# Probability-value products in runs of up to five key blocks, with the meta keys padded to 128

## The chip, the cores and the metric

One Trainium2 chip, one core used. The metric is the device time of one execution in microseconds (us). The profile is one execution of the same program, taken by the hardware profiler; times inside it count from the start of its span. Engines are PE (TensorE matmul), PEld (its weight loads), DVE (VectorE), ACT (ScalarE), POOL (GpSimd) and SP (which issues the DMAs).

## The reference, cut to what matters

Two layers of a streaming encoder. Each layer normalises, projects, runs three head groups (gated convolution, latent attention, RWKV-7) and projects back. Only the attention is touched here:

```
ckv_all = concat([ckv_past, rmsnorm(ckv)])            # KV_LORA = 128
kv = (ckv_all @ w_ukv).reshape(b, sk, 8, 64 + 64)      # per head: key part, value part
s = (q_nope . k_nope + q_rope . k_rope) * scale        # 8 heads
s = where(k_chunk <= q_chunk, s, -1e30)                # block-causal, chunks of 64
p = softmax(s)
o = p @ v                                              # 64 values per head
y_b = o * silu(gb)
```

The prompt has 16 meta tokens and 1024 frames. The sample has 64 new frames on 256 cached rows. Meta tokens and past are visible to every later query of their stream.

## The kernel before

Features lie on partitions and the 1104 tokens (64 sample, 16 meta, 1024 prompt) along the free axis. A layer has an input projection (`inproj`, `inproj_rest`), the attention and recurrence streams, and an output projection in two halves: `outproj_first` takes the first four of eight feature tiles, `outproj` the last four, which are the attention's.

Heads are taken in four pairs `pr`, queries in five units `u`: unit -1 holds the 64 sample and 16 meta queries, units 0 to 3 hold 256 prompt queries each. For a unit and each of its two heads:

- `scores` (L764) multiplies queries with keys into PSUM tiles `sc`. DVE takes the row maximum (`st`), ACT exponentiates into `p` (queries on partitions, keys along the free axis), DVE scales by the reciprocal of the sum.
- `transpose` (L831) turns `p` block by block so that keys lie on partitions. One block is one job of `jobs(u)` (L822): up to four PE transposes (two heads by two halves of the queries) into one PSUM tile `tr`, which `evict` (L665) copies to an SBUF tile `pt`, on ACT or DVE, whichever the planner has free sooner.
- `outputs` (L854) multiplies each `pt` with the value block `v` into the unit's only PSUM tile `po`: two matmuls per job, one per head, each with 64 columns of `v` as a 128x64 operand, into partitions 0 to 63 and 64 to 127. DVE then multiplies `po` with the gate into `yo`, and SP stores it to `yd`.

Unit u of the prompt has 2u + 3 jobs: the meta keys (16 partitions), 2u + 1 full blocks of 128 keys and a last block for the second half of the queries. Unit -1 has two. That makes 26 jobs a pair, 208 in both layers.

Which step comes next is decided when the program is built. `race` (L277) keeps the streams in the order `ORDER` = transpose, outputs, prepare, scores, and takes the first whose needs are met by the planner's clock; `fill` (`outproj_first`) goes where none is. `prepare` makes keys, values and queries of the pairs (`upk`, `val`, `upq`). A step's needs stand in its `yield`: tiles, PSUM tags, conditions. `outputs` yields once per job, as soon as one transposed tile waits. `transpose` may be ahead of `outputs` by fewer than `JOBS` = 3 tiles. `pt` tiles come from the ring `tmp` of four, which `qt` and `yraw` share. PSUM has two banks for `tr` (the 16-column score pieces use them too), one for `po`.

The trace puts all instructions on line L79, the helper that records every operation, so tiles tell them apart. An fp32 matmul stands in the trace as two PE rows, a transpose as one: a job of 256 queries is `tr` x4 and `po` x4.

Of the kernel before, what the change touches and what calls it, by code (L numbers as in the profile page):

```python
# [22 lines left out]
NMETA = 16  # L23
# [16 lines left out]
TURNS = ("sc", "tr", "sc", "tr", "po")  # L40
NEG = -1e30
PROBS = 8
JOBS = 3
LEAN = 0.1
POOL = 100.0
HOLD = 7
# [144 lines left out]
class Net:  # L191
# [421 lines left out]

    def value_tiles(self):
        vt = [self.S("x1", "v") for _ in range(2)]
        self.v = [vt[b < 4][:, 128 * (b % 4 if b < 4 else b - 4):128 * (b % 4 if b < 4 else b - 4) + 128] for b in range(12)]
        self.vs = lambda b, m: vt[b < 4][:, 128 * (b if b < 4 else b - 4):128 * ((b if b < 4 else b - 4) + m)]

# [89 lines left out]
    def attention(self, l):  # L708
# [6 lines left out]
        qa, keyed, valued, pt, turned, gates = {}, set(), set(), {}, [], {}  # L715
        count = {"scored": 0, "begun": 0, "p": 0, "out": 0, "jobs": 0}
# [105 lines left out]
        def jobs(u):  # L822

            if u < 0:
                n = PAD0
                return [[(0, 128, 0, n, 0, True, False), (1, 128, 2 * n, n, 0, False, False)], [(2, n, 0, n, 0, False, True)]]
            x = [[(3, NMETA, 0, 256, 0, True, False)]]
            x += [[(4 + k, 128, 0, 256, 0, False, False)] for k in range(2 * u + 1)]
            return x + [[(4 + 2 * u + 1, 128, 0, 128, 128, False, True)]]

        def transpose():  # L831
            for pr, u in units:
                yield (reached("scored", at[pr, u, 1] + 1),)
                ps2 = [pt[pr, u, j] for j in range(2)]
                q0, n = span(u)
                gates[pr, u] = self.small("gt", [128, 256], bufs=2)
                nc.sync.dma_start(gates[pr, u][:, :n], self.gd[2 + pr, :, q0:q0 + n])
                for js in jobs(u):
                    key = lambda b: (0, 128, PAST)[b] if u < 0 else 0 if b == 3 else NMETA + 128 * (b - 4)
                    yield lambda: len(turned) - count["jobs"] < JOBS, *ps2[0], *ps2[1], "tr"  # L840
                    ps = self.psa("tr", "tr")
                    for b, k, c, m, o, _, _ in js:
                        for j, p in enumerate(ps2):
                            for i, x in enumerate(p):
                                if o <= 128 * i:
                                    w, d = x.shape[0], c + j * m + 128 * i - o
                                    self.tr(ps[:k, d:d + w], x[:, key(b):key(b) + k], self.c(C_ID, w)[:w])
                    k, e = js[0][1], max(x[2] + 2 * x[3] for x in js)
                    t = self.tmp("pt")[:k, :e]
                    self.evict(t, ps[:k, :e])  # L850
                    turned.append(t)
                count["p"] -= len(ps2[0]) + len(ps2[1])

        def outputs():  # L854
            for pr, u in units:
                for x, js in enumerate(jobs(u)):
                    yield (lambda: len(turned) > count["jobs"] and all((pr, 4 * (b // 4) if b > 3 else 0 if b < 2 else b) in valued for b, *_ in js),)
                    t = turned[count["jobs"]]
                    yield t, *(self.v[b][:k] for b, k, *_ in js), *(("po",) if x == 0 else ())
                    if x == 0:  # L860
                        po = self.ps("po", "po")
                    for b, k, c, m, o, start, stop in js:
                        for j in range(2):
                            r = slice(64 * j, 64 * j + 64)
                            self.mm(po[r, o:o + m], self.v[b][:k, r], t[:, c + j * m:c + (j + 1) * m], start=start, stop=stop)
                    count["jobs"] += 1
                q0, n = span(u)
                yo = self.small("yo", [128, 256], bufs=2)
                nc.vector.tensor_tensor(out=yo[:, :n], in0=po[:, :n], in1=gates[pr, u][:, :n], op=ALU.mult)
                nc.sync.dma_start(self.yd[4 + pr, :, q0:q0 + n], yo[:, :n])  # L870
                count["out"] += 1
# [633 lines left out]
```

## Time and profile before

| | |
|---|---|
| median of 3 runs | 1581.6 us (1580.95 to 1582.13) |
| the profiled execution | 1581.68 us |
| its span | 1579.8 us |
| PE busy | 1522.3 us, 96% |
| DVE, ACT, POOL busy | 1040.9, 736.9, 276.2 us |
| granted TensorE clock, mean | 0.992 |

The attention streams' transposes and products run from 474 to 709 us in the first layer and from 1249 to 1483 us in the second. Before them lie the projections and the recurrence, behind them the second half of the output projection. PE is busy nearly all the time by its own rows, but the ends of matmuls are modelled and overlap, so a busy PE is not PE at its peak: the starts of the rows tell more than their durations. In a timeline row a run of like instructions is merged: its start, the time to its modelled end, and its count. In the rows by form, `128*64` is the weight operand's shape (partitions by columns), then comes the moving operand.

### The profile page before, as it was taken

The page shows a single profiled execution, that of the slowest core. Times are in us where ns is not written, and L with a number is a line of the kernel's source. Part 1 is how long each engine was busy: PE and PEld are TensorE (multiplying, and loading weights), DVE is VectorE, ACT ScalarE, POOL GpSimd, SP SyncE. Part 2 cuts the span into 40 slices and gives each one's busy share as a digit, 9 for nine tenths or more (in the row PEclk, how much of TensorE's full clock was granted, in tenths as well). Part 3 has the DMA queues.
Part 4 walks back from the last instruction along what each step waited for, and adds up shares of the span by engine and source line. Part 5 has one row for each costly group of instructions (what it writes and reads, how often), then busy time and mean ns, then how long its engine had stood idle before and what let it go on. Part 6 is the DMA issues. An engine that isn't in the chain of part 4 may idle for free. (4 is left out here: it accounts for less than half of the span.)

```text
span 1579.8 us, 31071 instructions
## 1 busy us (share of the span) xinstructions
PE 1522.3 (96%) x12304; PEld 1306.4 (83%) x12304; DVE 1040.9 (66%) x2591; ACT 736.9 (47%) x1730; POOL 276.2 (17%) x303
## 2 busy tenths in 40 slices
PE   7999999999999999999999999999999999999996
PEld 7988878888887767779999888798988867767896
DVE  7666575666758667755745675775666777666566
ACT  7135444324657556542522244434246666565342
POOL 0222222231211100100011222323122200100002
PEclk9999999999999999999999999999999999999998
DMA  6332122222224101112333312212312321012223
GB/s 213 121 102 77 42 66 51 76 47 87 77 85 144 36 25 32 58 45 87 128 108 101 108 43 53 81 38 72 67 47 93 120 93 45 17 32 68 69 64 115
DMA packets 95329, 119.84 MB, mean 76 GB/s; under 512 B 41872, under 2 KB 74768, under 8 KB 95184
## 3 DMA queue, kind: packets, MB, share of 16 engines
q1 hardware_dynamic: 95184, 117.87, 24.9%
q8 instruction: 96, 1.57, 0.4%
q14 instruction: 49, 0.40, 0.1%
HBM read 81.24 MB, written 36.60 MB: 75 GB/s over the span
## 5 line engine op out<-in xcount | busy, mean ns | idle before, releaser
L79 PE MATMUL prj<-hhi,whi 128*128 128x384 f32 (+1 forms) x1152 | 391.4, 340 | 7.4 <-ACT hhi L79 6.5
L79 PE MATMUL prj<-hhi,wlo 128*128 128x384 f32 (+1 forms) x1152 | 390.1, 339 | 0.9 <-DVE wlo L79 0.9
L79 PE MATMUL prj<-hlo,whi 128*128 128x384 f32 (+1 forms) x1152 | 387.7, 337 | 0.6 <-DVE hlo L79 0.6
L79 PEld LDWEIGHTS prj<-hhi,whi 128*128 128x128 f32 x1152 | 217.2, 189 | 12.5 <-ACT hhi L79 6.5
L79 PEld LDWEIGHTS prj<-hhi,wlo 128*128 128x128 f32 x1152 | 217.1, 188 | 6.1 <-DVE wlo L79 1.2
L79 PEld LDWEIGHTS prj<-hlo,whi 128*128 128x128 f32 x1152 | 217.4, 189 | 4.7 <-DVE hlo L79 1.0
L79 PE MATMUL prj<-yhi,wo 128*128 128x384 f32 (+2 forms) x776 | 199.4, 334 | 0.0
L79 ACT ACTIVATE p<-sc,st 128x144 f32<-128x144 f32 (+8 forms) x240 | 127.1, 536 | 79.3 <-DVE st L79 79.0
L79 PE MATMUL sc<-ka,qa 128*128 128x512 f32 (+9 forms) x720 | 150.5, 337 | 2.6 <-POOL qa L79 2.1
L79 PEld LDWEIGHTS prj<-yhi,wo 128*128 128x128 f32 x776 | 137.8, 188 | 2.6 <-issue 1.0
L79 DVE TENSOR_REDUCE st<-sc 128x1 f32<-128x144 f32 (+8 forms) x240 | 118.0, 501 | 23.0 <-PE sc L79 21.0
L79 PE MATMUL prj<-ylo,wo 128*128 128x384 f32 (+2 forms) x388 | 128.9, 332 | 0.0
L79 PEld LDWEIGHTS sc<-ka,qa 128*128 128x128 f32 (+1 forms) x720 | 112.0, 189 | 18.6 <-ACT p L79 3.6
L79 PE MATMUL tr<-cst,p 128*128 128x128 f32 (+3 forms) x752 | 122.0, 279 | 5.0 <-DVE p L79 4.3
L79 PEld LDWEIGHTS tr<-cst,p 128*128 128x128 f32 (+3 forms) x752 | 77.9, 132 | 51.8 <-issue 28.5
L79 ACT ACTIVATE pt<-tr 128x512 f32<-128x512 f32 (+4 forms) x158 | 84.6, 550 | 67.6 <-PE tr L79 66.7
L79 PE MATMUL po<-pt,v 128*64 128x256 f32 (+4 forms) x864 | 114.8, 365 | 0.9 <-DVE pt L79 0.8
L79 ACT ACTIVATE whi<-wraw 128x1024 fp32r<-128x1024 f32 x48 | 50.7, 1056 | 129.4 <-PE prj L79 119.8
L79 POOL TENSOR_TENSOR qa<-qt,qa 128x512 fp32r<-128x512 f32 (+1 forms) x40 | 48.0, 1211 | 350.3 <-ACT qa L79 261.7
L79 DVE TENSOR_TENSOR tri<-tri 48x14 f32<-48x14 f32 (+6 forms) x336 | 76.0, 226 | 17.1 <-DMA tri<-tri 7.3
L79 DVE TENSOR_SCALAR p<-p,st 80x336 f32<-80x336 f32 (+5 forms) x144 | 86.0, 600 | 1.4
L79 DVE TENSOR_TENSOR wlo<-wraw,whi 128x1024 fp32r<-128x1024 f32 x48 | 68.9, 1435 | 16.3 <-ACT whi L79 15.9
(223 smaller groups left out, 2606.8 us busy)
## 6 DMA issues: line engine op xcount, KB each, us to landing
wraw<-w_in SPq DMA_DIRECT2D x48, 512.0 KB, 3.7
wraw<-w_out SPq DMA_DIRECT2D x32, 256.0 KB, 2.6
zd<-z SPq DMA_DIRECT2D x14, 576.0 KB, 3.4
wr<-zd SPq DMA_DIRECT2D x36, 192.0 KB, 2.6
gd<-gate SPq DMA_DIRECT2D x12, 552.0 KB, 2.9
yraw<-yd SPq DMA_DIRECT2D x8, 552.0 KB, 4.0
xn<-x SPq DMA_DIRECT2D x8, 552.0 KB, 4.0
xd<-xn SPq DMA_DIRECT2D x8, 552.0 KB, 2.9
```

Of the source, the lines that this page charges most:

```text
L79: r = f(*args, **kw)
```

## The change

Four edits:

1. `outputs` no longer yields per job. The jobs of a unit are cut into batches of at most `BATCH` = 5, of near equal size (2; 3; 5; 4 and 3; 5 and 4 for the units -1 to 3), and a batch is issued in one run when all its transposed tiles and values are there.
2. The meta job transposes 128 columns of `p` instead of 16 and multiplies all 128 partitions with its value block.
3. `value_tiles` clears that value block once a layer (a POOL memset), so the 112 rows that are no meta keys add nothing.
4. `pt` gets a ring of its own of `JOBS` = 7 tiles, and `transpose` may be seven tiles ahead.

```
-JOBS = 3
+JOBS = 7
+BATCH = 5
...
         vt = [self.S("x1", "v") for _ in range(2)]
+        self.nc.gpsimd.memset(vt[1][:, 384:512], 0.0)
...
-            x = [[(3, NMETA, 0, 256, 0, True, False)]]
+            x = [[(3, 128, 0, 256, 0, True, False)]]
...
-                    t = self.tmp("pt")[:k, :e]
+                    t = self.small("pt", [128, 512], bufs=JOBS)[:k, :e]
...
-                for x, js in enumerate(jobs(u)):
-                    yield (lambda: len(turned) > count["jobs"] and all(... in valued for b, *_ in js),)
-                    t = turned[count["jobs"]]
-                    yield t, *(self.v[b][:k] for b, k, *_ in js), *(("po",) if x == 0 else ())
...
+                todo, po = jobs(u), None
+                while todo:
+                    size = -(-len(todo) // -(-len(todo) // BATCH))
+                    batch, todo = todo[:size], todo[size:]
+                    blocks = [b for js in batch for b, *_ in js]
+                    yield (lambda: len(turned) >= count["jobs"] + size and all(... in valued for b in blocks),)
+                    ts = turned[count["jobs"]:count["jobs"] + size]
+                    yield *ts, *(self.v[b][:k] for js in batch for b, k, *_ in js), *(() if po else ("po",))
+                    po = po or self.ps("po", "po")
+                    for t, js in zip(ts, batch):
+                        for b, k, c, m, o, start, stop in js:
...
+                    count["jobs"] += size
```

The program is built from this order, so the instructions of the attention stretch move on every engine. Ahead of the first attention unit the order is the old one.

PE before, first pair, unit 3: jobs of the long unit, where `tr` is a transposed block, `po` the unit's product, `p` the probabilities.

```order
L79 MATMUL po_5818<-pt_5777,v_5072 64x256 x2
L79 MATMUL tr_5821<-cst,p_5568 128x128
L79 MATMUL tr_5821<-cst,p_5598 128x128
L79 MATMUL tr_5821<-cst,p_5625 128x128
L79 MATMUL tr_5821<-cst,p_5716 128x128
L79 MATMUL po_5818<-pt_5784,v_5071 64x256 x2
L79 MATMUL tr_5830<-cst,p_5568 128x128
L79 MATMUL tr_5830<-cst,p_5598 128x128
L79 MATMUL tr_5830<-cst,p_5625 128x128
L79 MATMUL tr_5830<-cst,p_5716 128x128
L79 MATMUL po_5818<-pt_5816,v_5071 64x256 x2
```

Every transposed block is followed by one product; this goes on to the unit's last three, which stand together.

PE now, the same unit (its `po` has another number): the last block of the first batch, and the batch.

```order
L80 MATMUL tr_5912<-cst,p_5576 128x128
L80 MATMUL tr_5912<-cst,p_5674 128x128
L80 MATMUL tr_5912<-cst,p_5694 128x128
L80 MATMUL tr_5912<-cst,p_5727 128x128
L80 MATMUL po_5919<-pt_5783,v_5072 64x256 x2
L80 MATMUL po_5919<-pt_5790,v_5071 64x256 x2
L80 MATMUL po_5919<-pt_5831,v_5071 64x256 x2
L80 MATMUL po_5919<-pt_5849,v_5071 64x256 x2
L80 MATMUL po_5919<-pt_5895,v_5071 64x256 x2
```

Five products now stand in a row, the meta block's (`v_5072`) among them; the transposes of these blocks stand further ahead, among scores and fill.

PE now, a later unit of the fourth pair: `tr_7810` and `tr_7831` are given the same PSUM bank, `sc` are scores of another unit.

```order
L80 MATMUL tr_7810<-cst,p_7646 128x128
L80 MATMUL tr_7810<-cst,p_7666 128x128
L80 MATMUL tr_7810<-cst,p_7722 128x128
L80 MATMUL tr_7810<-cst,p_7742 128x128
L80 MATMUL sc_7846<-ka_4711,qa_7575 128x456
L80 MATMUL sc_7846<-ka_4712,qa_7575 128x456
L80 MATMUL sc_7846<-ka_4711,qa_7575 128x456
L80 MATMUL sc_7851<-ka_4711,qa_7575 128x456
L80 MATMUL tr_7831<-cst,p_7646 128x128
```

Between two tiles of one bank stand four score matmuls where before there stood another block's transposes and two products.

Counted in the whole program: `po` matmuls stand in 152 runs before (110 of them of one job) and in 70 now.

## Rows read from the trace of the kernel before

**Rows 1.** The page's first part: busy time and instructions of each engine.

```profile
PE 1522.3 (96%) x12304; PEld 1306.4 (83%) x12304; DVE 1040.9 (66%) x2591; ACT 736.9 (47%) x1730; POOL 276.2 (17%) x303
```

**Rows 2.** Busy time by stretch (both attentions): PE, PEld, DVE, ACT, POOL, clock, DMA.

```profile
480.00:700.00 220.00, 217.14 (x1528) 161.03 (x1527) 158.37 (x443) 130.91 (x367) 21.36 (x18) 0.99 0.18 55
1254.00:1474.00 220.00, 216.81 (x1527) 160.16 (x1527) 158.69 (x446) 131.24 (x368) 21.80 (x18) 1.00 0.18 55
```

**Rows 3.** Waits of PE, 474 to 709 us: total, times, longest.

```profile
PE tr L79 <- DVE p L79: 2.1, 4, 0.8
PE upq L79 <- ACT p L79: 1.3, 1, 1.3
PE sc L79 <- POOL qa L79: 0.9, 2, 0.6
PE po L79 <- DVE pt L79: 0.4, 1, 0.4
```

**Rows 4.** Timeline of all engines from 525.2 us: start, time, engine, operation, [idle before].

```profile
525.25 0.66 PE L79 MATMUL tr<-cst,p 128*128 128x128 f32 x4
525.83 0.20 PEld L79 LDWEIGHTS po<-pt,v 128*64 128x64 f32 x4 [0.17 <-issue]
525.83 0.65 PE L79 MATMUL po<-pt,v 128*64 128x256 f32 x4
525.94 0.60 ACT L79 ACTIVATE pt<-tr 128x512 f32<-128x512 f32 x1 [0.51 <-PE tr L79]
526.41 0.42 PEld L79 LDWEIGHTS tr<-cst,p 128*128 128x128 f32 x4 [0.39 <-issue]
526.42 0.66 PE L79 MATMUL tr<-cst,p 128*128 128x128 f32 x4
527.00 0.20 PEld L79 LDWEIGHTS po<-pt,v 128*64 128x64 f32 x4 [0.17 <-issue]
527.00 0.65 PE L79 MATMUL po<-pt,v 128*64 128x256 f32 x4
527.18 0.69 DVE L79 COPY pt<-tr 128x512 f32<-128x512 f32 x1 [1.69 <-PE tr L79]
```

**Rows 5.** Timeline of PE alone, five places: runs and what starts behind them.

```profile
487.93 1.23 PE L79 MATMUL po<-pt,v 16*64 16x256 f32 x8
489.09 0.52 PE L79 MATMUL sc<-ka,qa 128*128 128x264 f32 x2
...
499.76 1.49 PE L79 MATMUL sc<-ka,qa 128*128 128x456 f32 x6
501.09 0.20 PE L79 MATMUL sc<-hide 128*128 128x64 bf16 x1
501.22 0.87 PE L79 MATMUL po<-pt,v 128*64 128x256 f32 x8
502.02 0.50 PE L79 MATMUL sc<-ka,qa 128*128 128x16 f32 x3
...
518.24 0.82 PE L79 MATMUL tr<-cst,p 128*16 128x128 f32 x6
518.89 0.49 PE L79 MATMUL upk<-ckv,u 128*128 128x384 f32 x1
...
529.12 1.30 PE L79 MATMUL po<-pt,v 128*64 128x256 f32 x12
530.35 0.38 PE L79 MATMUL val<-u 128*128 128x128 f32 x1
```

**Rows 6.** Groups by form, whole span: count, busy us, mean ns, idle before.

```profile
L79 PE MATMUL tr<-cst,p 128*16 128x128 f32 x128 | 26.0, 273 | 2.5 <-DVE p L79 2.2
L79 PE MATMUL po<-pt,v 16*64 16x256 f32 x128 | 22.0, 400 | 0.0
L79 POOL MEMSET so<- 128x128 f32 x8 | 1.4, 203 | 0.0
```

**Rows 7.** The page's DMA issues: KB each, median us to landing.

```profile
wraw<-w_out SPq DMA_DIRECT2D x32, 256.0 KB, 2.6
```

More of the change, by code (lines that the diff above doesn't have):

```diff
@@ L855, in outputs @@
             for pr, u in units:
-                for x, js in enumerate(jobs(u)):
-                    yield (lambda: len(turned) > count["jobs"] and all((pr, 4 * (b // 4) if b > 3 else 0 if b < 2 else b) in valued for b, *_ in js),)
-                    t = turned[count["jobs"]]
-                    yield t, *(self.v[b][:k] for b, k, *_ in js), *(("po",) if x == 0 else ())
[L860 to L866, printed above, removed]
+                todo, po = jobs(u), None
[3 more added lines that the diff above has]
+                    blocks = [b for js in batch for b, *_ in js]
+                    yield (lambda: len(turned) >= count["jobs"] + size and all((pr, 4 * (b // 4) if b > 3 else 0 if b < 2 else b) in valued for b in blocks),)
+                    ts = turned[count["jobs"]:count["jobs"] + size]
[3 more added lines that the diff above has]
+                        for b, k, c, m, o, start, stop in js:
+                            for j in range(2):
+                                r = slice(64 * j, 64 * j + 64)
+                                self.mm(po[r, o:o + m], self.v[b][:k, r], t[:, c + j * m:c + (j + 1) * m], start=start, stop=stop)
+                    count["jobs"] += size
                 q0, n = span(u)
```

## The prediction

> **What bounds the kernel now.** I read the page's busy times first, then the stretches of the attention, then PE's waits there, then its timeline. PE is busy 96% of the span [rows 1]; in the two attention stretches it is 217 of 220 us, with the clock at 0.99 and 1.00, while DVE is busy 158 and ACT 131 [rows 2]. All waits of PE in the first layer's attention sum to 4.7 us [rows 3]. So PE's own order sets the time, and what is to be gained must lie inside "busy". The timeline shows where. A cycle of one transposed block and one product, from one `po` run to the next, takes 527.00 - 525.83 = 1.17 us [rows 4]. Read by starts, the same work needs less where like stands beside like: six transposes take 518.89 - 518.24 = 0.65, so 0.108 each and 0.43 for four; a run of three products (256, 256 and 128 queries) takes 530.35 - 529.12 = 1.23 and one of two (256 and 128) 502.02 - 501.22 = 0.80, so a product of 256 queries inside a run costs 0.43 [rows 5]. That makes 0.86. The missing 0.31 us is paid for going from transposes to products and back. The weight loads show it: in the cycle PEld idles 0.17 us before the `po` loads and 0.39 before the `tr` loads with nothing to wait for [rows 4]; elsewhere a load runs beside the matmul ahead of it.
>
> **The change, part by part.** The sum is made against the profiled execution, 1581.7 us, whose span is 1.9 us less; it agrees with the median of 1581.6.
>
> *Fewer runs.* The order has 152 runs of products before and 70 after. 82 x 0.31 = 25.4 us, all of it on PE's path, since nothing runs on PE in those holes. I use 0.31 for all of them, though it is read between two transposes; a run followed by scores could pay more or less, and there are 50 such runs before and 36 after.
>
> *Meta keys on 128 partitions.* Eight runs before hold a meta product followed by one of 128 partitions. Such a run of two takes 489.09 - 487.93 = 1.16 [rows 5]. A lone product takes 526.42 - 525.83 = 0.59 [rows 4], so a joined second one at 0.43 would make 1.02. The row of 16 partitions costs 0.14 when it touches one of 128: 8 x 0.14 = 1.1 us. With batches this would have been paid once in every prompt unit, 32 times; the padding avoids it. Its own price is nil: 16-column transposes take 273 ns against 0.108 us from start to start in both forms, and products of 16 partitions 400 ns by their rows, as long as the others [rows 5, 6]. The memset is one of 0.2 us a layer [rows 6], on POOL, which is busy 21 of 220 us [rows 2]. It waits for a slot that the last projection reads; behind it on POOL stand two gate multiplications, whose result is first read when a unit's product is ready, some 10 us into the attention.
>
> *Waits that the batch adds.* A product now waits for up to five copies instead of one. It is cheap, since four of the five are old: laid out with the distances above, the order leaves half of the tiles over 4 us between the last transpose and the product, against 2.5 before, and one under 1.2 us, against 22. PE's wait for such a copy is 0.4 us a layer now [rows 3]; I count no gain.
>
> *Waits at the banks of the transposes.* This is the price. Two blocks now follow each other without a product between. Between the runs of `tr_7810` and `tr_7831`, which share a bank, stand only four scores. Scores of 456 columns are 1.33 / 6 = 0.22 us apart [rows 5], so the bank is asked for 4 x 0.108 + 4 x 0.22 = 1.31 us after the first run began. Its copy ends 526.54 - 525.25 = 1.29 us after that on ACT and 527.87 - 526.42 = 1.45 on DVE, if the engine is free [rows 4]. Before, the next use came two cycles later, 2.34 us. Laid out so, 46 of 188 reuses now come less than 1.2 us after the last transpose of the tile before began; before, none did (least 1.27, half over 2.2). Each of the 46 waits for between nothing (by 1.29 against 1.31) and 0.60 us, when the copy stands behind another copy [rows 4]: 0 to 28 us. I take 0.1 us, near the lower end: the tile goes to the engine that the planner has free, ACT idles 40% and DVE 28% of the stretch [rows 2], and a wait that was paid gives the next copy time. 46 x 0.1 = 4.6 us.
>
> *What moves with it.* SP now issues four loads of attention output ahead of the projection weights of the sixth to eighth column, and they wait for the fourth pair's first two units. By the order those weights are first used 26 us or more after the product that holds the queue; a load lands in 2.6 us [rows 7]. It is hidden. Fill goes into the attention earlier, and less of it is left behind, but the amount is the same. Softmax steps keep their distance from their transposes.
>
> Sum: 1581.7 - 25.4 - 1.1 + 4.6 = 1559.8, about 1560 us.
>
> **The rivals.**
>
> *The copies take half of it.* DVE is the busiest engine behind PE, and two blocks in a row ask for two copies at once. If the 46 places wait midway between the bounds, 0.3 us, that is 14 us: 1581.7 - 26.5 + 14 = 1569. For it: 158 of 220 us on DVE, and copies stand in order behind exponentials and maxima. Against it: 61 us on DVE and 89 on ACT are free in a stretch [rows 2], and the moved copies are no more in number. The Trainium skill, TensorEngine Tiling (Array Packing), section Performance Considerations, says that a faster TensorE leaves PSUM evacuation as it was, and that the copy may become the bottleneck; this is that rival, and the 4.7 us of waits in the rows do not yet show it.
>
> *Slower.* PE takes its queue in order. When a transpose waits for its bank, the scores behind it wait too, DVE and ACT get their rows later, and the copies that stand behind those come later still. If this spreads from the 46 places to all 188 reuses, it decides from 26.5 / 188 = 0.14 us each. At 0.25 it costs 47 us and gives 1602. For it: both copy engines also carry the softmax. Against it: PE leads DVE and ACT by idle time on both, and the waits now are of single steps, not of chains [rows 3].
>
> *The hole is paid per product, not per run.* Then joining saves nothing and the time stays at 1580 to 1583. Against it speak the runs of three and of two [rows 5]: a joined product costs 0.43, which is all that a product takes. In the same way each score or value matmul that the builder sets between the products of a batch opens the hole again; the 70 runs (56 batches) already count these.
>
> Larger gain: if no copy is late and runs ahead of scores paid 0.05 us more than those ahead of transposes, the time is 1581.7 - 26.5 - 0.05 x 14, about 1554.5; a little more if the waits of [rows 3] fall away.
>
> **How the numbers follow.** Forecast, 1551 to 1566: 0.70. Copies take half, 1566 to 1578: 0.17. No change (the hole paid per product, or waits that eat the gain): 0.05. Slower, 1585 and above: 0.07. Gain of more than 31 us: 0.01. The range for 8 in 10 takes the forecast and the better part of the second case: 1551 to 1572. What a measurement can tell from no change is about 0.2%, 3 us: faster 0.88, same 0.05, slower 0.07.
>
> **What would show it.** Right: `po` in about 70 runs; runs of five products of 256 queries of some 0.15 + 5 x 0.43 = 2.3 us; PEld's idle time before `tr` and `po` loads less than half; the attention stretches shorter by some 4 to 7 us each and what follows by 5 to 8, since more of the fill lies inside; PE's waits there up from under 5 us to 6 to 8 a layer, nearly all new ones of `tr` for `pt`. Wrong: `tr` waiting for copies for over 13 us a layer (then the second case), `sc` and `upq` waiting as well (the third), or a joined product at more than 0.5 us (the fourth).

## The result and the profile after

The changed kernel takes 1568.4 us (median; 1567.1 to 1569.8) against 1581.9 for the kernel before on the same chip: a ratio of 0.991, interval 0.9898 to 0.9921. It is 13.5 us faster; 21.6 us were forecast. The time lies inside the range, but above the band of the forecast itself (1551 to 1566) and in the one that was given to late copies (1566 to 1578). The direction held, and so did the mechanism of the gain; nearly two fifths of the gain did not come.

The profiled execution of after took 1569.75 us, its span 1568.0. Its busy times, to be read beside [rows 1]:

```profile
PE 1507.0 (96%) x12304; PEld 1320.1 (84%) x12304; DVE 1029.5 (66%) x2569; ACT 745.1 (48%) x1752; POOL 276.5 (18%) x305
```

PE executes the same number of instructions and is 15.3 us less busy. 22 instructions have moved from DVE, 11.4 us less busy, to ACT, 8.2 us more. So the gain lies where it was sought, in the order of PE's instructions. The same two stretches as in [rows 2] (PE, PEld, DVE, ACT, POOL busy, clock, DMA share, GB/s):

```profile
480.00:700.00 220.00, 215.18 (x1563) 172.54 (x1562) 156.29 (x439) 137.86 (x384) 21.06 (x18) 1.00 0.21 62
1254.00:1474.00 220.00, 216.02 (x1550) 171.97 (x1549) 154.59 (x430) 137.65 (x381) 19.29 (x16) 1.00 0.20 62
```

More matmuls fit into the same 220 us (1563 and 1550 against 1528 and 1527), PEld is busier and PE a little less. A run of five products, from the timeline of PE (start, time to the modelled end, operation, count):

```profile
527.27 0.38 PE L80 MATMUL tr<-cst,p 128*128 128x128 f32 x2
527.58 2.38 PE L80 MATMUL po<-pt,v 128*64 128x256 f32 x20
529.89 0.87 PE L80 MATMUL tr<-cst,p 128*128 128x128 f32 x6
```

It takes 529.89 - 527.58 = 2.31 us; predicted were 0.15 + 5 x 0.43 = 2.3. The trace has `po` in 70 runs.

What the weight loads waited for, whole span (total us, times, longest). First before:

```profile
PEld tr L79 <- issue: 28.5, 77, 0.6
PEld po L79 <- issue: 23.9, 131, 0.4
PEld tr L79 <- DVE p L79: 7.1, 12, 1.4
PEld sc L79 <- ACT p L79: 3.6, 12, 0.7
PEld tr L79 <- ACT pt L79: 3.4, 9, 0.5
PEld sc L79 <- POOL qa L79: 3.4, 5, 0.9
```

And after:

```profile
PEld tr L80 <- ACT pt L80: 10.1, 31, 0.7
PEld po L80 <- issue: 8.7, 38, 0.4
PEld tr L80 <- issue: 8.2, 32, 0.4
PEld sc L80 <- POOL qa L80: 5.9, 7, 1.1
PEld sc L80 <- ACT p L80: 4.2, 10, 0.9
PEld tr L80 <- DVE p L80: 3.9, 5, 1.6
```

"issue" is idle time with nothing to wait for that the profile shows, the hole of [rows 4]. It falls from 52.4 to 16.9 us. Waits with a name change places: `tr` for a copy out of its bank (`ACT pt`) is 6.7 us more and scores for `qa` 2.5 more, `tr` for probabilities on DVE 3.2 less. Over all loads of the attention (`tr`, `po`, `sc`, `upq`, `upk`, `val`) the named waits do not rise: 36.5 us before, 32.7 after. How much of a load's wait is lost time these rows do not tell; PE's own rows have 2.1 us of `tr` for `ACT pt` in the whole span. PE's own waits in the first layer's attention, to be read beside [rows 3], and then those in the second's (1248 to 1483 us):

```profile
PE sc L80 <- POOL qa L80: 1.7, 3, 0.7
PE upq L80 <- ACT p L80: 1.3, 1, 1.3
PE tr L80 <- DVE p L80: 1.2, 2, 0.6
PE sc L80 <- DVE ka L80: 0.9, 1, 0.9
PE tr L80 <- ACT pt L80: 0.6, 2, 0.3
```

```profile
PE sc L80 <- POOL qa L80: 1.7, 3, 0.7
PE tr L80 <- ACT pt L80: 1.6, 4, 0.5
PE sc L80 <- ACT p L80: 0.5, 1, 0.5
PE tr L80 <- ACT p L80: 0.2, 1, 0.2
```

With the smaller ones the first layer has 7.0 us (4.7 before), the second 4.0 (4.8 before).

Where the time went by stage: from the first `po` to the last, the attentions took 225.3 and 227.1 us before and 227.9 and 229.3 after. They did not become shorter. What follows did: from the last product of the first layer to the first of the second 546.8 became 539.8, and from the last product of the second layer to PE's last instruction 86.8 became 78.2. The time won inside the attention was filled with projection work (314 projection matmuls between the first and the last `po` of the two layers, 210 before), and the gain appears where that work is missing afterwards.

### The profile page after: what moved, and what is told of

It is laid out like the page before. It is cut to its first block, busy times and chain, and to the rows that moved or that the text cites. A ratio compares the mean times of both kernels' runs of the same rounds, so it can differ in the third digit from the quotient of the medians.

```text
span 1568.0 us, 31064 instructions
## 1 busy us (share of the span) xinstructions
PE 1507.0 (96%) x12304; PEld 1320.1 (84%) x12304; DVE 1029.5 (66%) x2569; ACT 745.1 (48%) x1752; POOL 276.5 (18%) x305
## 5 line engine op out<-in xcount | busy, mean ns | idle before, releaser
L80 PE MATMUL prj<-yhi,wo 128*128 128x384 f32 (+2 forms) x776 | 207.9, 339 | 0.0
L80 PE MATMUL sc<-ka,qa 128*128 128x456 f32 (+9 forms) x720 | 152.4, 335 | 5.7 <-POOL qa L80 3.7
L80 DVE TENSOR_REDUCE st<-sc 128x1 f32<-128x456 f32 (+8 forms) x240 | 118.6, 503 | 34.4 <-PE sc L80 33.2
L80 ACT ACTIVATE pt<-tr 128x512 f32<-128x512 f32 (+3 forms) x174 | 92.7, 558 | 58.2 <-PE tr L80 57.3
L80 PE MATMUL tr<-cst,p 128*128 128x128 f32 (+2 forms) x752 | 113.8, 279 | 5.1 <-DVE p L80 2.6
L80 PEld LDWEIGHTS tr<-cst,p 128*128 128x128 f32 (+2 forms) x752 | 82.2, 141 | 27.1 <-ACT pt L80 10.1
L80 PE MATMUL po<-pt,v 128*64 128x256 f32 (+3 forms) x864 | 99.9, 355 | 0.1
L80 PEld LDWEIGHTS po<-pt,v 128*64 128x64 f32 (+1 forms) x864 | 56.6, 136 | 32.9 <-issue 8.7
L80 DVE TENSOR_SCALAR p<-p,st 80x336 f32<-80x336 f32 (+5 forms) x144 | 82.8, 575 | 1.5
```

The lines of the kernel that those rows point to most:

```text
L80: r = f(*args, **kw)
```

## The experiments

Each kernel below was timed beside the kernel before, whose median was 1581.7 to 1582.3 us in these runs. The table puts the orders, the times and the traces side by side; all but the first three columns are in us, as differences to before.

- Runs, torn pairs and tight reuses are counted in the order. A torn pair is a break between the two half-width matmuls of one product. A tight reuse is a transposes' bank asked for less than 1.2 us after the last transpose of its last tile began, when the order is laid out with the distances that neighbours have in the trace of before (a few more or less, by how pairs that stand nowhere in that trace are priced).
- "Due" is what the prediction's prices give: 0.31 for each run more or less than 152, 0.14 for each change of row count inside a run (8 before), 0.1 for each tight reuse. "Came" is the difference of the medians.
- The last four columns are from the profiled executions. Each PE row is given the time until the next row starts, and the rows are added up by tile. A wait is booked on the row ahead of the one that waits, and a change of shape partly on the row ahead of it.

| kernel | runs | torn pairs | tight reuses | due | came | products `po` | transposes `tr` | scores `sc` | projection `prj` |
|---|---|---|---|---|---|---|---|---|---|
| before (us, not differences) | 152 | 2 | 0 | | | 104.4 | 98.6 | 152.2 | 865.9 |
| e5: no batch, three tiles | 168 | 6 | 8 | +4.7 | +7.9 | +2.5 | +2.4 | +0.8 | +0.4 |
| e1: no batch, seven tiles | 117 | 12 | 2 | -11.8 | -3.9 | -2.3 | -2.0 | +0.6 | +0.7 |
| after | 70 | 14 | 46 | -21.9 | -13.5 | -9.4 | -10.1 | -0.2 | +8.2 |
| e2: meta keys on 16 | 70 | 14 | 43 | -17.7 | -7.9 | -3.9 | -12.0 | +0.9 | +7.2 |
| e8: third bank | 69 | 20 | 18 | -25.0 | -6.8 | -7.9 | -8.9 | +3.4 | +8.9 |
| e10: whole batches | 58 | 2 | 48 | -25.4 | -16.8 | -15.4 | -12.2 | +3.2 | +9.1 |
| e6: whole threes | 72 | 2 | 32 | -22.7 | -19.5 | -13.3 | -14.9 | +2.7 | +9.5 |
| e3: later transposes | 62 | 4 | 48 | -24.2 | -5.0 | -13.2 | -14.3 | +7.7 | +16.4 |

Every kernel falls short of what is due, by 3 us (e5, e6) to 19. The profiled executions lie up to 3.3 us (e6) from their medians, so differences of that size between the last columns mean nothing.

**Undoing the batch and the ring.** In both kernels each batch is one job; the padding stays. The first edit is in both kernels, the second in e5 alone.

```
-BATCH = 5
+BATCH = 1
...
-JOBS = 7
+JOBS = 3
```

> The changed kernel with BATCH = 1 and JOBS = 3: padding, memset and a ring of its own for pt stay, the batches and the depth go. Its order has 168 runs of products (152 in the kernel before, 8 of them with a change of shape inside; 70 in the changed one). Theory (the gain is the runs that are saved, 0.31 us each): no gain, 168 - 152 = 16 runs more at 0.31 and 8 shape changes fewer at 0.14, +3.9 us, so 1583 to 1588. Rival (the gain comes from the padding or from pt no longer sharing its ring): 1568 to 1572.

> The changed kernel with BATCH = 1 alone: the ring of seven stays, a product goes when one block is ready. Its order has 117 runs. Theory (runs): 117 - 70 = 47 runs more than the changed kernel at 0.31 = 14.6 us, less up to 6 us of waits at the transposes' banks, which only 2 of 188 reuses now press: 1577 to 1583. Rival (transposing further ahead is what gains, not the batch): 1568 or less.

Measured: 1590.2 us (ratio 1.0051, 1.0036 to 1.0066) with three tiles, 1578.5 (0.9978, 0.9969 to 0.9988) with seven. The first is above its theory's 1583 to 1588 and far from the rival's 1568 to 1572, the second inside its theory's 1577 to 1583. The padding and the ring of its own bring nothing by themselves: the order has 168 runs, 16 more than before, at 0.31 us 5.0 of the 8 us that it is slower. The deeper ring cuts the runs to 117 and gives 11.8 us, where 51 x 0.31 = 15.8 were due by the count. The batch cuts them to 70 and gives 10.1 us, where 47 x 0.31 = 14.6 were due. So fewer runs are the gain, in both steps, and both steps lose about a quarter or a third of it. The weight loads' waits at seven tiles without a batch:

```profile
PEld po L80 <- issue: 16.5, 95, 0.4
PEld tr L80 <- issue: 13.8, 38, 0.8
PEld tr L80 <- ACT pt L80: 10.4, 27, 0.8
```

The wait for the copies is as long there as in after (10.1), though only 2 reuses are tight. By the table e1 falls short of what is due by 8 us, as after does, so the shortfall isn't a matter of the batches alone. Whether these waits are that shortfall the row doesn't tell: PE's own rows in e1 have 0.8 us of it.

**Meta keys on 16 partitions.**

```
-            x = [[(3, 128, 0, 256, 0, True, False)]]
+            x = [[(3, NMETA, 0, 256, 0, True, False)]]
```

> The changed kernel with the meta job on 16 partitions as before. 70 runs, but 32 of them hold one change of tile shape. Theory (a change of shape inside a run costs 0.14 us): 32 x 0.14 = 4.5 us, 1573 (1571 to 1575). Rival (the shape change costs nothing inside a run, or the padded transposes cost as much): 1568.

Measured: 1574.4 us (0.9951, 0.9935 to 0.9968), 6.0 more than after, inside the theory's range. The run of five in its timeline (the merged row bears the form of its first product, the meta one; the other four have 128 rows):

```profile
528.99 2.52 PE L80 MATMUL po<-pt,v 16*64 16x256 f32 x20
531.44 0.76 PE L80 MATMUL tr<-cst,p 128*128 128x128 f32 x5
```

531.44 - 528.99 = 2.45 us against 2.31, the 0.14 of the forecast. 32 of them make 4.5 of the 6.0 us. The padding is worth its place in the kernel with batches; before, only 8 such places stood in the order.

**A third bank for the transposes.** They also take banks of the recurrence, which until then went to the scores alone.

```
-SOLO = {"sc": ("sc", "rw"), "tr": ("tr",), "fill": ("rs",)}
+SOLO = {"sc": ("sc", "rw"), "tr": ("tr", "tr", "rw"), "fill": ("rs",)}
```

> The changed kernel with every third transposed tile in a bank of rw, which scores then share (SOLO tr = tr, tr, rw). 69 runs. 18 instead of 46 reuses come within 1.2 us. Theory (the gain that is missing went into waits of tr for the copies, PEld tr for ACT pt 10.1 us against 3.5 before): these waits fall to 3 to 5 us and the time to 1561 to 1565. Rival (the missing gain went to scores and queries that wait for softmax and POOL): 1567 to 1570, with the waits of tr lower and those of sc higher.

Measured: 1575.6 us (0.9962, 0.9947 to 0.9977), 7 more than after: both theories missed the time. Tight reuses fell from 46 to 18, and the wait for copies fell with them, from 10.1 to 6.0, but others rose:

```profile
PEld sc L80 <- ACT p L80: 8.0, 18, 1.0
PEld sc L80 <- POOL qa L80: 7.0, 8, 1.2
PEld tr L80 <- DVE p L80: 6.9, 12, 1.9
PEld tr L80 <- ACT pt L80: 6.0, 17, 0.6
```

`sc` for `ACT p` is probably the same thing at the scores' banks: the exponential that must have read them. It rose from 4.2 to 8.0 us, `tr` for `p` from 3.9 to 6.9, and the scores' rows cost 3.6 us more than in after. So a bank taken from the scores moved the waits, as the rival had it. It is not the whole of the 7 us: the order also has 20 torn pairs instead of 14, and what a torn pair costs is read below (0.57 us).

**Whose hole is it?** The kernel before, with products in the 128x128 shape of the transposes: all 128 value columns are multiplied for each head, and the head's half is taken at the gate.

```
-                        self.mm(po[r, o:o + m], self.v[b][:k, r], t[...], start=start, stop=stop)
+                        d = 256 * j + o
+                        self.mm(po[:, d:d + m], self.v[b][:k], t[...], start=start and j == 0, stop=stop and j == 1, ...)
...
-                nc.vector.tensor_tensor(out=yo[:, :n], in0=po[:, :n], in1=gates[pr, u][:, :n], op=ALU.mult)
+                for j in range(2):
+                    r = slice(64 * j, 64 * j + 64)
+                    nc.vector.tensor_tensor(out=yo[r, :n], in0=po[r, 256 * j:256 * j + n], in1=gates[pr, u][r, :n], op=ALU.mult)
```

> The kernel before (no batches, three transposed tiles), but each product computes all 128 value columns for each head, and the head's half is taken at the gate multiplication, so that a product has the 128x128 shape of the transposes instead of two 128x64 halves side by side. The products' own time doubles: 78.3 us as counted from their columns, +78.3. Theory (the hole of 0.31 us belongs to the change from full-width to half-width products): no hole is left, 152 x 0.31 = 47 us are saved: 1582 + 78 - 47 = 1613 (1605 to 1620), and the weight load idles before transposes and products with nothing to wait for fall to a few us a layer. Rival (the hole belongs to going from transposes to products at all): 1660 (1652 to 1668).

Measured: 1635.9 us (1.0337, 1.0322 to 1.0353), outside both ranges and between them. The rows decide for the theory:

```profile
534.77 1.03 PE L79 MATMUL po<-pt,v 128*128 128x256 f32 x4
535.64 0.38 PE L79 MATMUL tr<-cst,p 128*128 128x128 f32 x2
535.86 1.03 PE L79 MATMUL po<-pt,v 128*128 128x256 f32 x4
```

A product between transposes takes 535.64 - 534.77 = 0.87, twice the 0.43 of a joined product, and two transposes take 0.22, as anywhere; nothing is left over. The idle time "issue" in the first layer's attention tells the same:

```profile
PEld po L79 <- issue: 1.8, 11, 0.2
PEld tr L79 <- issue: 1.7, 6, 0.3
```

12.0 and 14.8 us stood there before. So the hole belongs to the change of the array's shape from 128x128 to 128x64 and back, not to going from transposes to products. The Trainium skill, TensorEngine Tiling (Array Packing), section Key Properties, says that a change of the tiling mode drains TensorE; these rows agree as to when time is lost, with 0.31 us for the way there and back; the drain itself no row shows. The total missed by 23 us. By the starts, as in the table, products grew by 62 us, transposes gained only 14 and the projection lost 7. Part of it are meta products, 1.06 us instead of 0.87 since their 16 rows are a change of shape again; the rest is not settled.

**Batches kept whole.** In the order of after, 12 batches are torn, by 14 tears in the middle of a pair: the framework's scheduler, which comes after the planner, sends half products ahead, most often the first one alone. In the timeline of PE in after:

```profile
559.45 0.65 PE L80 MATMUL po<-pt,v 128*64 128x256 f32 x2
560.02 1.51 PE L80 MATMUL sc<-ka,qa 128*128 128x456 f32 x6
561.37 0.20 PE L80 MATMUL sc<-hide 128*128 128x64 bf16 x1
561.41 0.94 PE L80 MATMUL sc<-ka,qa 128*128 128x512 f32 x3
562.28 2.16 PE L80 MATMUL po<-pt,v 128*64 128x256 f32 x18
564.37 0.33 PE L80 MATMUL tr<-cst,p 128*128 128x128 f32 x1
```

The experiment pins the first product of a batch behind the PE work that was written ahead of it.

```
     def mm(self, out, lhs, rhs, start, stop, group=True):
-        self.nc.tensor.matmul(out, lhs, rhs, start=start, stop=stop, skip_group_check=not group)
+        i = self.nc.tensor.matmul(out, lhs, rhs, start=start, stop=stop, skip_group_check=not group)
+        if self.first:
+            self.tc.keep_in_program_order(i)
+        self.first = False
...
+                    self.first = True
                     for t, js in zip(ts, batch):
```

> The kernel after, with the first product of each batch held behind the TensorE work written ahead of it. In the kernel after, 12 batches stand torn in the order, each in the middle of a pair of half-width products: the first half product went ahead by itself and scores or transposes stand between. Here 58 runs of products instead of 70. Theory: each tear costs a hole of 0.31 us, and up to 0.43 us more because the two halves of a pair no longer run side by side, 12 x 0.31 = 3.7 to 12 x 0.74 = 8.9 us: 1559.5 to 1564.5 against 1568.4. Rival: the early half filled time in which TensorE would have waited anyway; then no change, 1567 to 1570.

Measured: 1565.2 us (1560.6 to 1566.9; 0.9885, 0.9866 to 0.9904), 3.2 less than after, just short of the theory's bound of 3.7 and outside the rival's range. The same batch there:

```profile
562.60 2.17 PE L80 MATMUL po<-pt,v 128*64 128x256 f32 x20
564.70 0.66 PE L80 MATMUL tr<-cst,p 128*128 128x128 f32 x4
```

The whole batch takes 564.70 - 562.60 = 2.10 us, the torn one's remainder 564.37 - 562.28 = 2.09. The half product that went ahead, 560.02 - 559.45 = 0.57, is lost entirely: half a pair beside nothing costs as much as the pair. Two tears are left; 12 x 0.57 = 6.8 us. The products' rows fall by 6.0 (95.0 to 89.0 over the span), the transposes' by 2.1, and the scores' rise by 3.4 and the others by 1.9. So the tears are a real cost, and more than half of what their removal saves is lost at other rows. The prediction had charged each piece with 0.31; by that price 12 runs less are worth 3.7 us, so e10 falls as far short of what is due as after does.

**Shorter batches, and later transposes.** Both with batches kept whole. The first two edits are e6's, the third is e3's.

```
-JOBS = 7
-BATCH = 5
+JOBS = 5
+BATCH = 3
...
-        return self.last(ring[0]) + 0.25 if len(ring) >= bufs else 0.0
+        return self.last(ring[0]) + (0.45 if tag == "tr" else 0.25) if len(ring) >= bufs else 0.0
```

> As e10_whole_batches, but batches of up to three blocks and a ring of five transposed tiles: 72 runs of products instead of 58, and 32 reuses of a transposes' bank within 1.2 us instead of 48. Theory (a run costs 0.31, a tight reuse about 0.1): +4.3 - 1.6 = 2.7 us more than e10_whole_batches, about 1564 if that gives 1561. Rival (the waits that longer batches make at the banks, of the scores too, are dear, 0.3 us and more for each tight reuse): not slower than e10_whole_batches, -0.5 us or less.

> As e10_whole_batches, but the planner lets transposes have a bank 0.20 us later after its last use: 62 runs, 48 reuses within 1.2 us as there, but half of all reuses come after 2.42 us or more instead of 1.92. Theory (runs decide, the waits are small): +1.2 us for four more runs, up to +4 by the distances of the order: 1562 to 1566 if e10_whole_batches gives 1561. Rival (the waits of transposes for copies are what was lost): 3 to 6 us faster than e10_whole_batches.

Measured: 1562.5 us (1562.4 to 1565.9; 0.9872, 0.9856 to 0.9889) for threes. By the theory it should have lost 2.7 us; it gained 2.7, as far as runs this close tell the two apart. It falls short of what is due by only 3 us, where fives kept whole fall short by 9. The rival forecast that time, but its cause, 16 tight reuses fewer, is not shown: e6 also lets the transposes run only five tiles ahead instead of seven. e1, with seven tiles and 2 tight reuses, falls short by 8, and e5, with three tiles, by 3. That speaks rather for how far the transposes run ahead; threes with seven tiles were not run, and the two are not told apart. `tr` for `ACT pt` is 3.3 us in e6, against 9.4 with fives, and `tr` for `p` 7.2 against 3.7.

Later transposes: 1577.0 us (0.9969, 0.9956 to 0.9982), 11.8 more than fives kept whole, against both theories (1562 to 1566, and 3 to 6 faster). Its rows:

```profile
PEld tr L80 <- DVE p L80: 13.4, 19, 1.8
PEld sc L80 <- ACT p L80: 6.7, 16, 1.2
PEld tr L80 <- ACT pt L80: 6.1, 18, 0.8
PEld sc L80 <- POOL qa L80: 5.4, 7, 0.9
```

A fifth of a microsecond more room at the banks shifts the whole order: `tr` waits for probabilities instead (3.7 to 13.4). From the first `po` to the last its attentions take 237.0 and 237.1 us, 12 and 11 more than with fives kept whole, and only part of that is missing behind them. Room that the planner leaves for the copies did not pay here.

**Is the plan's price of a run at fault?** The planner charges 0.087 us for leaving a run of half-width products; the trace shows 0.31 for both ways. Four kernels ask what an honest price would do: the first edit is in all four, the second in e14 alone.

```
-            cost += 0.087 if self.small and not small else 0.0
+            cost += 0.31 if self.small and not small else 0.0
...
-LEAN = 0.1
+LEAN = 0.4
```

> As e6_whole_threes, but the planner charges 0.31 us instead of 0.087 for the way out of a run of half-width products, as the traces show it. 72 runs, 32 reuses within 1.2 us, both as there; the order alone, laid out with the distances of the kernel before, is 3.5 us shorter. Theory (much of the lost gain are waits that arise since the plan's clock of TensorE runs ahead of the real one, so that work is put where its input is not ready): the waits do not rise and the time falls by 3 to 7 us from e6_whole_threes, 1555 to 1560. Rival (the waits are made by the softmax and the copies, whatever the plan charges): what the order saves comes back as waits, 1561 to 1564.

> As e10_whole_batches (batches of five kept whole), with the same price of 0.31 us in the planner: 58 runs, 58 reuses within 1.2 us instead of 48, the order alone 2.7 us shorter. Theory (the plan's clock): 1557 to 1562. Rival (waits made by softmax and copies; ten more tight reuses at 0.1 to 0.3 us): 1564 to 1568.

> The kernel before with the price of 0.31 us in the planner and nothing else: 146 runs of products instead of 152, 8 reuses within 1.2 us instead of none; the order alone is 7.8 us shorter. Theory (the plan's clock): 1570 to 1576. Rival (waits eat what the order saves): 1578 to 1583.

> As e11_priced_threes, but a copy of a transposed block goes to ScalarE already when VectorE is free up to 0.4 us earlier, instead of 0.1: 72 runs, 30 reuses within 1.2 us, half of the reuses after 2.40 us or more instead of 2.16, and by the distances of the order 2.1 us less. Theory (the copies wait on the busier VectorE): 2 to 5 us faster than e11_priced_threes. Rival (ScalarE's exponentials come later for it, and transposes and scores wait for probabilities instead): the same as e11_priced_threes or slower.

Measured: 1586.3 us (1.0026, 1.0011 to 1.0040), 1587.7 (1.0038, 1.0026 to 1.0051), 1609.8 (1.0176, 1.0160 to 1.0192) and 1588.8 (1.0044, 1.0029 to 1.0059). The first three lie 24, 23 and 28 us above their partners (e6, e10 and before), far outside both theories. The stages show why this edit can't answer its question. The first `po` of the second layer begins at 1273.6 us in e11 against 1249.6 in e6. Of these 24 us, 10.7 are lost by the first `po` of the first layer (495.4 against 484.7) and 19.0 between the two attentions (558.7 against 539.7); the first attention is 5.6 shorter. The recurrence also has half-width products, and the price applies to them too. Where it runs beside the input projection, that projection's rows, counted by starts, take 28, 23 and 27 us more than in the partners: its order became worse. From the second layer's first `po` on, to PE's last instruction, e11 takes 302.2 us against 304.2, e12 303.7 against 304.6 (e10) and e13 313.7 against 313.9. By that part alone the price is worth 0 to 2 us, where the theory wanted 3 to 7 over both layers. This leans to the rival. It is not settled, since a version that prices the attention alone was not tried, and the profiled execution of e12 was 5.5 us faster than its median. e14 is 2.5 us slower than e11, and more copies on ScalarE did not shorten the wait for them (`tr` for `ACT pt` 7.0 us against 2.1 in e11). The time is as its rival had it; `tr` and `sc` for `p`, which by the rival should have risen, are 11.6 us against 12.0.

## Why the prediction was right or wrong

*Fewer runs, -25.4.* Right in its mechanism. The hole belongs to the change of shape (the full-width kernel), it is paid per run and not per product (2.31 us for five), and each step that takes runs away gains. The third rival, a price per product, is out. With batches kept whole, products and transposes together are 27.6 us cheaper, where 94 runs less and the padding made 30.2; in after they are 19.5 cheaper, where 26.5 were due. Part of the difference is torn pairs. The term charged each piece 0.31, as any run; a tear in the middle of a pair costs 0.57, since it also ends the pair's concurrency. 12 more of them than before, at 0.26, are 3.1 us.

*Meta keys, -1.1.* The price is right, 0.14 us a place; 6.0 us when it is undone in the batches, where 4.5 were due. The 1.1 us themselves no run shows apart.

*Waits for copies that the batch adds, nothing.* Right: the loads of `po` have no wait for `pt` of any size in after, 1.3 and 0.9 us in before.

*Waits at the banks, +4.6.* The rows allow this size and do not fix it: `tr` for `ACT pt` is 2.1 us in PE's own rows (none before) and 6.7 us more in the loads' rows. The place that the prediction worked out stands in the trace of after (PE, PEld and ACT in one timeline; in brackets the idle time before):

```profile
684.83 0.66 PE L80 MATMUL tr<-cst,p 128*128 128x128 f32 x4
685.24 1.08 PE L80 MATMUL sc<-ka,qa 128*128 128x456 f32 x4
685.52 0.60 ACT L80 ACTIVATE pt<-tr 128x512 f32<-128x512 f32 x1
686.17 0.42 PEld L80 LDWEIGHTS tr<-cst,p 128*128 128x128 f32 x4 [0.24 <-ACT pt L80]
686.17 0.66 PE L80 MATMUL tr<-cst,p 128*128 128x128 f32 x4
```

Four transposes, four scores, and the bank again at 686.17 - 684.83 = 1.34 us, where 1.31 were asked for and 1.29 possible.

*Everything else, nothing.* This is the step that was mis-sized. The sum took the scores and the projection to cost what they had cost: "the amount is the same". The starts say otherwise. The projection's rows take 874.1 us instead of 865.9, 8.2 more for the same matmuls (6.8 of it at the output projection, whose matmuls moved), and the scores' rows in e10 and e6, with whole batches, 3 more than before. Between the first and the last `po` stand 104 more projection matmuls and cost 24.2 us more there (40.5 to 64.7); outside, 104 fewer save only 16.0. Without batches (e5, e1) the projection's rows change by 0.7 us at most. What makes a projection matmul dearer there is not told apart: at the 0.19 us that one cost inside the attention before, 4 of the 8 us are explained by the place alone; the other 4 may be waits of the scores and transposes behind it, and some of the time may only be booked from the row ahead to the projection. PE's own waits do not show it: 11.0 us in the two attentions, 9.5 before.

So of the 8 us that did not come, 3 are torn pairs, priced too low. The other 5 are open. They show at the projection's rows, but e1 falls short by as much without that rise, and no single run takes them away: the third bank and the later transposes lowered one named wait and raised others.

*The rivals.* "The copies take half of it" is the time that came (1569), but not its mechanism as written: its sign, over 13 us a layer of `tr` waiting for copies, stayed away (10.1 us in both together). That the stated range held is in part luck, since it took in the better part of this rival's band. "Slower" was named with scores and `upq` waiting as its sign. Such waits did rise a little in the loads' rows (scores for `qa` 2.5 us, for `p` 0.6, `upq` for `p` 0.9), and the kernel was faster all the same.

*The signs.* Right: 70 runs and 2.3 us for five. Half right: PE's waits of 6 to 8 us a layer (7.0 in the first, 4.0 in the second), and what follows the attentions 5 to 8 us shorter (7.0 and 8.6). Wrong as worded: that PEld's idle time before `tr` and `po` loads would fall to less than half. It fell from 86.0 to 60.0 us; only the part without a named wait did (52.4 to 16.9), and before `po` loads alone the whole hardly moved (34.2 to 32.9). Wrong: that nearly all new waits would be `tr` for `pt` (0.6 of the 7.0, 1.6 of the 4.0), and that the attentions would be 4 to 7 us shorter each. They became 2 us longer: all of the gain is taken out as projection work done earlier.

## What to carry to other kernels

Grouping products of one array shape paid here per change of shape that it removed, and such a change can be priced from two places in a trace, a run and a lone one. Of that gain a good third did not come. Before trusting the sum, price what the moved work pushes elsewhere as well as the moved work itself: here the filling work went into the attention, and by the starts its rows then cost some 7 us more over the whole span. Time from start to start, added up by tile, shows this; busy times and named waits did not. Try a shorter group and a shallower ring too: three at a time with five tiles, kept whole, is the fastest measured (1562.5 us, a ratio of 0.987). After a scheduler has had its way, look for groups torn in the middle.

## What the runs showed of the hardware

- Half of a pair of 128x64 products by itself costs 0.57 us, the pair 0.59 [rows 4]; in a run, a pair costs 0.43.
- The hole of a run of half-width products between transposes is 0.31 us, and nothing is left of it when the products are full-width: 0.87 us, twice 0.43.
- 16 partitions of a product beside 128 cost 0.14 us in a half-width run, and 1.06 - 0.87 = 0.19 us among full-width ones.
